# Layer 0 of a hybrid decoder step: a plain first chunk of 256 tokens, and the Strassen weight sums of the second chunk on GpSimd

## The chip, the cores and the metric

The kernel runs on one core of a Trainium2 chip. The metric is the device time of one execution in microseconds (us). Of the kernel before three runs are shown; their median counts. The engines are TensorE (PE in the profile, its weight loads PEld), VectorE (DVE), ScalarE (ACT), GpSimd (POOL) and SyncE (SP), which here only issues DMAs, in order.

## The reference

The step has two layers over 4096 prompt tokens and 8 sample tokens of width 1024. Only layer 0 is touched. It is, in short:

```python
def even_layer(x, pool_prefix, conv_prefix, pos0, g_norm, w_in, pool_w, pool_scale, conv_w, w_out):
    h = rms_norm(x, g_norm)                       # x * rsqrt(mean(x*x) + eps) * g_norm
    p = jnp.einsum('btd,de->bte', h, w_in)        # 1024 -> 3072
    u, z_a, b_gate, c_gate, v_in, z_b = jnp.split(p, EVEN_SPLITS, axis=-1)
    d = pool_mix(u, pool_prefix, pos0).reshape(B, T, N_POOL_GROUPS, POOL_GROUP)   # windows 2, 4, 8, 16
    y_a = jnp.einsum('btgc,gce->btge', d, pool_w).reshape(B, T, W_POOL) * pool_scale * jax.nn.silu(z_a)
    v = c_gate * v_in
    y_b = b_gate * short_conv(v, conv_prefix, conv_w) * jax.nn.silu(z_b)
    y = jnp.einsum('bte,ed->btd', jnp.concatenate([y_a, y_b], axis=-1), w_out)
    return x + y, new_pool, new_conv
```

Layer 1 is sliding-window attention with its own projections. All is float32.

## The kernel before, in words

Every float32 operand of a product is split in two float32r parts, high and low (`split`: ScalarE copies the high part, VectorE subtracts), and a product takes three matmuls: high by high, high by low, low by high.

Layer 0 takes the tokens in chunks (`L0_CHUNKS`): 768, 768, 768, 768, 512, 512; the 8 samples ride with the first. For each chunk:

- `prep` loads the token tiles, normalizes them (`x_norm0`: ScalarE squares, GpSimd makes the root, VectorE scales), turns them by TensorE transposes and makes the seven token operands of a Strassen-Winograd product: B11, B21, B22 and the sums T1 to T4, split in `bh`, `bl`, `th`, `tl`. It works in rounds of 256 tokens; the two halves of a chunk are the two columns of the Strassen square.
- `mixers` runs 12 pairs of output blocks of 128 channels (4 groups, 3 pairs each). A pair is 7 products of 4 x 3 matmuls with half the chunk's tokens as columns: 84 matmuls of 384 columns (388 in chunk 0, 256 in the small chunks). Its weight operands are A11, A12 (one block), the sums S1 to S4, and A22, 3.5 tiles of 128x1024 to be split per pair. In chunk 0 `operands` loads both blocks from `w_in`, GpSimd multiplies them by the norm's gains (`scaled`), VectorE makes three sums and GpSimd one, and all seven are written to a scratch tensor `wsc`; later chunks load them from there. Between the products stand the evictions, the pooling, the convolution and the gates, on VectorE, ScalarE and, for small copies, GpSimd.
- `outproj` multiplies by `w_out` in 8 weight blocks: 3 x 8 x 2 matmuls of 512 columns for every 128 tokens, adds the input and writes the result for layer 1.

Raw weight tiles (`wr`), high parts (`wh`) and low parts (`wl`) have three buffers each, token tiles and weight sums share two (`x`), the operands of a chunk and its `yh`, `yl` have one. A scheduler orders the instructions of each engine at build time by their dependences and its own estimates; so `prep` of the next chunk, which stands between `mixers` and `outproj` in the code, comes out mixed with the output projection. Layer 1 follows from 1498 us on.

Of the kernel before, what the change touches and what calls it, by code (L numbers as in the profile page):

```python
# [54 lines left out]
def hybrid_kernel(  # L55
# [94 lines left out]
    with ExitStack() as l1:  # L150
# [119 lines left out]
        def x_norm0(xt, n, junk):  # L270
# [4 lines left out]
            dve.tensor_scalar(out=xt[:n], in0=xt[:n], scalar1=r[:n, 0:1], scalar2=None, op0=ALU.mult)  # L275

        def prep(ci):
# [39 lines left out]
            for i in range(np2):  # L317
                xs = []
                for j in (1, 0):
                    if early:  # L320
                        xt = early.pop(0)
                    else:
                        xt = xp.tile([P, D], F32, tag="x", name="xt", bufs=2)
                        r0 = t0 + j * (n // 2) + i * P
# [12 lines left out]
                operand_cols(i * P, P, quad)  # L337
            if ci == 0:
                xs1 = xp.tile([P, D], F32, tag="x", name="xs1", bufs=2)
                sp.dma_start(xs1[:NS], xs_flat)  # L340
                sj = xp.tile([P, KT, P], F32, tag="x", name="sj", bufs=2)
                x_norm0(xs1, NS, sj)
                v = samples_to_channels(xs1, pt)
                h = NS // 2
                operand_cols(n // 2, h, lambda k, j: v[:, 4 * k:4 * k + 4, j * h:j * h + h])
            return bh, bl, th, tl

        def mixers(ci, X, yh, yl):
            t0, n = L0_CHUNKS[ci]
            L = n // 2  # L350
            hs = NS // 2 if ci == 0 else 0
            w = L + hs
            bh, bl, th, tl = X
            B = {"B11": (bh, bl, 0), "B21": (bh, bl, 1), "B22": (bh, bl, 2), "T1": (th, tl, 0),
                 "T2": (th, tl, 1), "T3": (th, tl, 2), "T4": (th, tl, 3)}
# [46 lines left out]
            WX = w  # L402

            def put_y(kt, pi, fn):
                y = tp.tile([P, WX], F32, tag="dy", name="y")
# [1 line left out]
                cs = slice(pi * L, pi * L + L)
                split(yh[:, kt, cs], yl[:, kt, cs], y[:, :L])
                if hs:
                    ss_ = slice(n + pi * hs, n + pi * hs + hs)  # L410
                    split(yh[:, kt, ss_], yl[:, kt, ss_], y[:, L:w])

            for g in range(4):
                win = 2 << g
                us = [tp.tile([P, 15 + WX], F32, tag="uv", name="u") for _ in range(2)]
# [8 lines left out]

                def pooled(pi):
# [985 lines left out]
```

## Time and profile before

| | |
|---|---|
| median of 3 runs | 3348.16 us (3347.56 to 3349.6) |
| profiled execution, its own time | 3354.14 us |
| its span, first to last instruction | 3352.4 us |
| TensorE busy | 3131.0 us, 93% |
| VectorE busy | 2471.7 us, 74% |
| ScalarE busy | 1892.4 us, 56% |
| GpSimd busy | 860.1 us, 26% |
| mean granted TensorE clock | 0.981 |

TensorE is the busiest engine, so a change pays where TensorE waits, or where it is given less or faster work. A busy share over the whole span hides that: layer 0 has stretches with TensorE at over 99% and others at a quarter. So the rows further down cut layer 0 where TensorE turns from one kind of work to the next. Matmul durations overlap, since they are pipelined; what a matmul costs is the length of a full stretch divided by its matmuls.

### The profile page before, as it was taken

The numbers are of one execution on the slowest core, as the hardware profiler recorded it, in microseconds if no ns is written. First come the engines' busy times: TensorE is split into PE (matmuls) and PEld (weight loads), VectorE is DVE, ScalarE is ACT, GpSimd is POOL, SyncE is SP. The second block draws the span as 40 slices with busy tenths as digits, with TensorE's granted clock in tenths as the row PEclk, the third lists the DMA queues.
The fourth block names the chain that finished last, engine by engine and source line by source line (L and its number), as shares of the span: only waits on it lengthen the run. The fifth ranks groups of instructions, "written<-read, shape, count | busy, mean of one in ns | idle before, by whom it ended". The sixth has DMA issues, their size and how long they took to land.

```text
span 3352.4 us, 48712 instructions
## 1 busy us (share of the span) xinstructions
PE 3131.0 (93%) x16362; PEld 2687.0 (80%) x16362; DVE 2471.7 (74%) x4914; ACT 1892.4 (56%) x4277; POOL 860.1 (26%) x1219
## 2 busy tenths in 40 slices
PE   4889999999999999998989999999999999999877
PEld 3887898898899898976767777777787777776665
DVE  5896467467467486853897987979979788797863
ACT  4334345245244254544686876858858688585761
POOL 2441011011011011110333442534425334243420
PEclk9999999999999999999999999999999999999988
DMA  4554444534543555553213324233242242322212
GB/s 135 173 170 140 149 123 134 160 120 129 164 126 121 171 176 180 176 176 111 88 53 103 113 76 138 73 103 114 74 138 79 89 128 71 120 70 63 70 64 98
DMA packets 220997, 398.90 MB, mean 119 GB/s; under 512 B 25257, under 2 KB 89393, under 8 KB 220706
## 3 DMA queue, kind: packets, MB, share of 16 engines
q1 hardware_dynamic: 220745, 395.78, 37.6%
q8 instruction: 129, 2.11, 0.3%
q14 instruction: 123, 1.00, 0.1%
HBM read 339.70 MB, written 58.31 MB: 119 GB/s over the span
## 4 chain that ended last, share of the span: by engine, by line
PE 23%; DVE 15%; ACT 7%; DMA 5%; issue 3%; POOL 1%; SPq 1%; DVEq 0%; ACTq 0%; POOLq 0%
PE pst L720 6%; PE pst L721 6%; PE pst L722 6%; ACT s L989 3%; DVE wl L688 2%; DMA wr<-in_w_in_odd_dram 2%; DVE qt L72 1%; PE o L1023 1%; DVE s L973 1%; DMA xr<-x 1%; PE sc L965 1%; DMA out_dram<-xr 1%; DVE st L983 1%; DVE ot L75 1%; ACT wh L687 1%
## 5 line engine op out<-in xcount | busy, mean ns | idle before, releaser
L69 ACT ACTIVATE wh<-wr 128x512 fp32r<-128x512 f32 (+1 forms) x392 | 327.6, 840 | 448.5 <-PE pz L373 125.0
L72 DVE TENSOR_TENSOR wl<-wr,wh 128x512 fp32r<-128x512 f32 (+1 forms) x392 | 373.2, 960 | 214.9 <-ACT wh L69 194.0
L688 DVE SCALAR_TENSOR_TENSOR wl<-wr,gt,wh 128x256 fp32r<-128x256 f32 (+1 forms) x448 | 277.3, 637 | 69.5 <-ACT wh L687 67.5
L687 ACT ACTIVATE wh<-wr,gt 128x256 fp32r<-128x256 f32 (+1 forms) x448 | 250.3, 596 | 120.6 <-DMA wr<-in_w_in_odd_dram 80.3
L720 PE MATMUL pst<-wh,hh 128*128 128x512 f32 x768 | 312.0, 406 | 1.7 <-DVE xr L75 1.7
L722 PE MATMUL pst<-wl,hh 128*128 128x512 f32 x768 | 304.4, 396 | 0.0
L721 PE MATMUL pst<-wh,hl 128*128 128x512 f32 x768 | 304.2, 396 | 0.0
L373 PE MATMUL px<-th,wh 128*128 128x384 f32 (+2 forms) x864 | 280.1, 324 | 9.8 <-DVE za L75 6.4
L373 PE MATMUL px<-th,wl 128*128 128x384 f32 (+2 forms) x864 | 278.7, 323 | 0.0
L373 PE MATMUL px<-tl,wh 128*128 128x384 f32 (+2 forms) x864 | 278.7, 323 | 0.0
L1009 POOL TENSOR_SCALAR_AFFINE_SELECT qh<-ph 128x512 fp32r<-128x512 f32 x124 | 88.7, 715 | 692.5 <-ACT ph L69 675.4
L989 ACT ACTIVATE s<-s,st,rq 128x128 f32<-128x128 f32 x512 | 246.8, 483 | 33.8 <-DVE st L985 32.3
L808 PE MATMUL psz<-hh,wh 128*128 128x512 f32 x512 | 213.5, 417 | 9.8 <-ACT wh L687 9.8
L720 PE MATMUL pst<-wh,yh 128*128 128x512 f32 x512 | 211.2, 413 | 2.6 <-DVE xr L75 2.6
L570 PE MATMUL pso<-who,yh 128*128 128x512 f32 x512 | 204.7, 400 | 5.6 <-DVE xr L75 5.5
L809 PE MATMUL psz<-hl,wh 128*128 128x512 f32 x512 | 208.7, 408 | 0.0
L810 PE MATMUL psz<-hh,wl 128*128 128x512 f32 x512 | 207.6, 405 | 0.0
L721 PE MATMUL pst<-wh,yl 128*128 128x512 f32 x512 | 204.3, 399 | 0.0
L572 PE MATMUL pso<-who,yl 128*128 128x512 f32 x512 | 204.3, 399 | 0.0
L722 PE MATMUL pst<-wl,yh 128*128 128x512 f32 x512 | 204.2, 399 | 0.0
L574 PE MATMUL pso<-wlo,yh 128*128 128x512 f32 x512 | 202.7, 397 | 0.0
L428 POOL COPY ucar<-u 128x15 f32<-128x15 f32 x48 | 26.4, 550 | 611.0 <-DVE u L75 599.2
(327 smaller groups left out, 9038.6 us busy)
## 6 DMA issues: line engine op xcount, KB each, us to landing
wr<-wsc SPq DMA_DIRECT2D x180, 512.0 KB
wr<-in_w_in_odd_dram SPq DMA_DIRECT2D x320, 256.0 KB
wr<-in_w_out_odd_dram SPq DMA_DIRECT2D x128, 256.0 KB
wro<-in_w_out_even_dram SPq DMA_DIRECT2D x48, 512.0 KB
xr<-in_x_prompt_dram SPq DMA_DIRECT2D x64, 256.0 KB
x<-xr SPq DMA_DIRECT2D x64, 256.0 KB
xt<-x SPq DMA_DIRECT2D x32, 512.0 KB
xr<-x SPq DMA_DIRECT2D x64, 256.0 KB
```

The lines of the kernel that those rows point to most:

```text
L69: return act.activation(out, in_, AF.Copy)
L72: return dve.tensor_tensor(out=out, in0=a, in1=b, op=ALU.subtract)
L373: pe.matmul(ps, lhsT=u_[:, at, kt, :], rhs=v_[:, o, kt, :], start=start and kt == 0 and i == 0, stop=kt == 3 and i == 2, skip_group_check= ...
L687: act.activation(wh[ix], raw[ix], AF.Copy, scale=gt[:, kt:kt + 1])
L688: dve.scalar_tensor_tensor(out=wl[ix], in0=raw[ix], scalar=gt[:, kt:kt + 1], in1=f(wh[ix]), op0=ALU.mult, op1=ALU.subtract)
L720: pe.matmul(acc[i], lhsT=xh(kt), rhs=wh, start=kt == 0, stop=False)
L721: pe.matmul(acc[i], lhsT=xl(kt), rhs=wh, start=False, stop=False)
L722: pe.matmul(acc[i], lhsT=xh(kt), rhs=wl, start=False, stop=kt == KT - 1)
L808: pe.matmul(acc[e], lhsT=wh[:, k, es], rhs=xh, start=kt == 0, stop=False)
L809: pe.matmul(acc[e], lhsT=wh[:, k, es], rhs=xl, start=False, stop=False)
L810: pe.matmul(acc[e], lhsT=wl[:, k, es], rhs=xh, start=False, stop=kt == KT - 1)
L989: C["exp"] = act.activation(s[:, h, :], s[:, h, :], AF.Exp, bias=nm[:, h:h + 1], scale=r4[:, h:h + 1], accum_out=den[:, h:h + 1])
```

## The change

The chunks become one of 256 tokens and five of 768. The first chunk, with the samples, is a plain product: no Strassen operands, 24 weight blocks of 24 matmuls each with 264 columns, 576 in place of 1008 of half width. Its split tokens, its y and the samples' strip all lie in the buffers of `yh` and `yl`, so `bh`, `bl`, `th`, `tl` stay free for chunk 1. The norm's gains go to the tokens instead of the weights: a tile `gb` holds them for every partition, and `x_norm0` multiplies by both in one scalar_tensor_tensor. The second chunk makes the weight sums, all four on GpSimd, and writes only these to `wsc`; the blocks themselves are loaded from `w_in` in every chunk.

```diff
-L0_CHUNKS = [(0, 768), (768, 768), (1536, 768), (2304, 768), (3072, 512), (3584, 512)]
+L0_CHUNKS = [(0, 256)] + [(256 + 768 * i, 768) for i in range(5)]
...
-        wsc = [dram.tile([P, 7, 4, P], F32, tag=f"wsc{i}", name=f"wsc{i}") for i in range(12)]
+        wsc = [dram.tile([P, 4, 4, P], F32, tag=f"wsc{i}", name=f"wsc{i}") for i in range(12)]
...
-        g0 = c1.tile([P, KT], F32, tag="g0", name="g0")
+        gb = c1.tile([P, D], F32, tag="gb", name="gb")
...
-        def scaled(raw):
-            v = raw.rearrange("p a k e -> p (a k) e")
-            pool.tensor_tensor(out=v, in0=v, in1=g0.unsqueeze(2).to_broadcast([P, KT, P]),
-                               op=ALU.mult)
-
         first_w = []
 
+        def block_parts(eb):
+            return parts(first_w.pop(0) if first_w else load_block(eb))
+
         def operands(ci, pair, blocks):
 
-            if ci > 0:
-                out = []
-                for i in range(4):
+            ra = load_block(blocks[0])
+            ga = parts(ra)
+            if ci > 1:
+                out = [ga]
+                for i in range(2):
                     raw = raw_tile()
-                    n = 1 if i == 3 else 2
-                    sp.dma_start(raw[:, :n], wsc[pair][:, 2 * i:2 * i + n])
-                    out.append(parts(raw[:, :n]))
+                    sp.dma_start(raw, wsc[pair][:, 2 * i:2 * i + 2])
+                    out.append(parts(raw))
+                raw = raw_tile()
+                e0 = blocks[1] * P
+                sp.dma_start(raw[:, 0], w_in[:, 4:8, e0:e0 + P])
+                out.append(parts(raw[:, 0:1]))
                 return out
-            ra = first_w.pop(0) if first_w else load_block(blocks[0])
-            scaled(ra)
-            ga = parts(ra)
-            rb = first_w.pop(0) if first_w else load_block(blocks[1])
-            scaled(rb)
+            rb = load_block(blocks[1])
             s12 = xp.tile([P, 2, 4, P], F32, tag="x", name="s12", bufs=2)
             s34 = xp.tile([P, 2, 4, P], F32, tag="x", name="s34", bufs=2)
-            add(s12[:, 1], rb[:, 0], rb[:, 1])
-            sub(s12[:, 0], s12[:, 1], ra[:, 0])
+            pool.tensor_tensor(out=s12[:, 1], in0=rb[:, 0], in1=rb[:, 1], op=ALU.add)
+            pool.tensor_tensor(out=s12[:, 0], in0=s12[:, 1], in1=ra[:, 0], op=ALU.subtract)
+            gs12 = parts(s12)
             pool.tensor_tensor(out=s34[:, 0], in0=ra[:, 0], in1=rb[:, 0], op=ALU.subtract)
-            sub(s34[:, 1], ra[:, 1], s12[:, 0])
-            sp.dma_start(wsc[pair][:, 0:2], ra)
-            gs12 = parts(s12)
-            sp.dma_start(wsc[pair][:, 2:4], s12)
+            pool.tensor_tensor(out=s34[:, 1], in0=ra[:, 1], in1=s12[:, 0], op=ALU.subtract)
+            sp.dma_start(wsc[pair][:, 0:2], s12)
             gs34 = parts(s34)
-            sp.dma_start(wsc[pair][:, 4:6], s34)
-            gb_ = parts(rb[:, 1:2])
-            sp.dma_start(wsc[pair][:, 6:7], rb[:, 1:2])
-            return [ga, gs12, gs34, gb_]
+            sp.dma_start(wsc[pair][:, 2:4], s34)
+            return [ga, gs12, gs34, parts(rb[:, 1:2])]
...
             r = rstd(ss[:n], n, 1, 1.0 / D, EPS, sm, "rn")
-            dve.tensor_scalar(out=xt[:n], in0=xt[:n], scalar1=r[:n, 0:1], scalar2=None, op0=ALU.mult)
+            dve.scalar_tensor_tensor(out=xt[:n], in0=xt[:n], scalar=r[:n, 0:1], in1=gb[:n],
+                                     op0=ALU.mult, op1=ALU.mult)
+
+        def prep0():
+
+            n = L0_CHUNKS[0][1]
+            both = [yp.tile([P, KT, 2 * (n + NS) + 40], F32R, tag=t, name=f"{t}0") for t in ("yh", "yl")]
+            hh, hl = (t[:, :, 0:n + NS] for t in both)
+            yh, yl = (t[:, :, n + NS:2 * (n + NS)] for t in both)
+            ysk = both[0][:, :, 2 * (n + NS):]
+            for i in range(n // P):
+                xt = early[i]
+                x_norm0(xt, P, yl[:, :, 0:P])
+                to_channels(xt, pt, hh, hl, i * P)
+            x_norm0(early[-1], NS, yl[:, :, P:2 * P])
+            v = samples_to_channels(early[-1], pt)
+            split(hh[:, :, n:n + NS], hl[:, :, n:n + NS], v)
+            return hh, hl, yh, yl, ysk
...
+                if plain:
+                    for e in range(2):
+                        wh, wl = block_parts(blocks[e])
+                        ps = bank("ps")
+                        for kt in range(KT):
+                            for k, (u_, v_) in enumerate(((wh, hh), (wh, hl), (wl, hh))):
+                                pe.matmul(ps, lhsT=u_[:, kt // 4, kt % 4, :], rhs=v_[:, kt, :],
+                                          start=kt == 0 and k == 0, stop=kt == KT - 1 and k == 2)
+                        if e == 0:
+                            out11(ps, None)
+                            if mid is not None:
+                                mid()
+                    return ps
...
         early = []
-        for i, r0 in enumerate((384, 0)):
+        for i in range(2):
             xt = xp.tile([P, D], F32, tag="x", name="xe", bufs=2)
-            sp.dma_start(xt, xp_flat[r0:r0 + P, :])
+            sp.dma_start(xt, xp_flat[i * P:(i + 1) * P, :])
             early.append(xt)
-        with nc.allow_non_contiguous_dma(reason="per-channel gains"):
-            sp.dma_start(g0, norm_g[0].rearrange("(k p) -> p k", p=P))
-        first_w += [load_block(0), load_block(4)]
-        nxt = prep(0)
+            if i == 0:
+                sp.dma_start(gb, norm_g[0].partition_broadcast(P))
+                first_w.append(load_block(0))
+        xs1 = wp.tile([P, D], F32, tag="wr", name="xs1", bufs=3)
+        sp.dma_start(xs1[:NS], xs_flat)
+        early.append(xs1)
+        first_w.append(load_block(4))
+        hh, hl, yh0, yl0, ysk0 = prep0()
         setup()
```

The remaining edits make one list entry of two where the chunk is plain (`NP`), and copy from PSUM where there is no second summand.

At the head, VectorE's first rows before were (`xe`, `xt` token tiles, `rnr` the root, `wr` a raw weight tile, `bl`, `tl` low parts):

```order
L275 TENSOR_SCALAR xe<-xe,rnr 128x1024 x2
L72 TENSOR_TENSOR wl<-wr,wh 128x1024
L72 TENSOR_TENSOR bl<-tr,bh 128x4x128
L72 TENSOR_TENSOR t_190<-b_176,tr 128x512
L72 TENSOR_TENSOR bl<-tr,bh 128x4x128
L72 TENSOR_TENSOR t_199<-tr,t_190 128x512
L72 TENSOR_TENSOR tl<-t_190,th 128x4x128
L72 TENSOR_TENSOR bl<-tr,bh 128x4x128
```

and now, where `xs` are the samples and the split tokens lie in `yh`, `yl`:

```order
L72 TENSOR_TENSOR wl<-wr,wh 128x1024
L271 SCALAR_TENSOR_TENSOR xe<-xe,rnr,gb 128x1024 x2
L271 SCALAR_TENSOR_TENSOR xs_156<-xs_156,rnr,gb 8x1024
L72 TENSOR_TENSOR yl_161<-tr,yh_160 128x4x128
L72 TENSOR_TENSOR wl<-wr,wh 128x1024
L72 TENSOR_TENSOR yl_161<-tr,yh_160 128x4x128 x2
L72 TENSOR_TENSOR pwl<-pw,pwh 128x512
L72 TENSOR_TENSOR yl_161<-tr,yh_160 128x4x128
L72 TENSOR_TENSOR yl_161<-trs,yh_160 128x8x8
L75 TENSOR_TENSOR nx<-u 128x270
```

The first weight block's split stands ahead of the scaling now, and three scalings and the splits of two tiles make the whole of it; before, two more rounds of eleven operations follow.

At the start of the output projection TensorE's rows before were (`tr` transposes of the next chunk's tokens, `pso` outputs of the projection, `who`, `wlo` its split weights):

```order
L574 MATMUL pso<-wlo,yh 128x512
L570 MATMUL pso<-who,yh 128x512
L334 MATMUL tr<-ident,xt 128x128 x4
L572 MATMUL pso<-who,yl 128x512
L574 MATMUL pso<-wlo,yh 128x512
L570 MATMUL pso<-who,yh 128x512
L572 MATMUL pso<-who,yl 128x512
L574 MATMUL pso<-wlo,yh 128x512
L570 MATMUL pso<-who,yh 128x512
L572 MATMUL pso<-who,yl 128x512
L574 MATMUL pso<-wlo,yh 128x512
```

and now, a few rows further on, where 4 + 6 + 4 + 12 + 4 + 1 + 4 + 17 such matmuls and transposes lie behind (`pss` are the samples):

```order
L592 MATMUL pso<-who,yh_160 128x512
L594 MATMUL pso<-who,yl_161 128x512
L596 MATMUL pso<-wlo,yh_160 128x512
L344 MATMUL tr<-ident,xt 128x128 x32
L601 MATMUL pss<-who,yh_160 40x512
L603 MATMUL pss<-wlo,yh_160 40x512
L601 MATMUL pss<-who,yh_160 40x512
L603 MATMUL pss<-wlo,yh_160 40x512
L601 MATMUL pss<-who,yh_160 40x512
L603 MATMUL pss<-wlo,yh_160 40x512
L601 MATMUL pss<-who,yh_160 40x512
```

Before, transposes alternate with some ten output matmuls all the way; now the last two rounds' 32 transposes stand in one run, and the samples' and the remaining output matmuls follow them.

On GpSimd the weight work of the chunk that makes the sums was, in chunk 0 (`wr` scaled by `g`, `s` a sum, `vv`, `u` tiles that get a few carried columns):

```order
L197 TENSOR_TENSOR wr<-wr,g_139 128x1024 x2
L221 TENSOR_TENSOR s_612<-wr 128x512
L197 TENSOR_TENSOR wr<-wr,g_139 128x1024
L496 COPY vv<-vcar 128x2
L221 TENSOR_TENSOR s_782<-wr 128x512
L197 TENSOR_TENSOR wr<-wr,g_139 128x1024
L497 COPY vcar<-vv 128x2
L496 COPY vv<-vcar 128x2
L497 COPY vcar<-vv 128x2
```

and is now, in chunk 1:

```order
L218 TENSOR_TENSOR s_1656<-wr 128x512
L221 TENSOR_TENSOR s_1657<-wr 128x512
L219 TENSOR_TENSOR s_1656<-s_1656,wr 128x512
L222 TENSOR_TENSOR s_1657<-wr,s_1656 128x512
L218 TENSOR_TENSOR s_1806<-wr 128x512
L221 TENSOR_TENSOR s_1807<-wr 128x512
L219 TENSOR_TENSOR s_1806<-s_1806,wr 128x512
L222 TENSOR_TENSOR s_1807<-wr,s_1806 128x512
L449 COPY ucar<-u 128x15
L448 COPY u<-ucar 128x15
L449 COPY ucar<-u 128x15
L218 TENSOR_TENSOR s_1960<-wr 128x512
```

The scaling is gone, a pair has four sums instead of one, and the sums of two pairs run before the first copy that waits for a product. On SP the second state load, `sc_raw`, now has two loads of weight blocks right behind it, and the two copies of the caches stand among the weight loads of the first chunk; before, these copies were issued at 33.34 and 42.12 us, ahead of the products.

## Rows read from the trace of the kernel before

**Rows 1.** Busy time of each engine by stretch, cut where TensorE's work changes.
```profile
core 0: us, PE busy (x) PEld busy (x) DVE busy (x) ACT busy (x) POOL busy (x), PEclk, DMA share, GB/s
0.00:53.50 53.50, 13.38 (x56) 9.92 (x56) 30.27 (x43) 24.27 (x43) 14.88 (x44) 1.00 0.53 167
77.50:92.20 14.70, 5.04 (x16) 2.88 (x16) 9.41 (x14) 3.78 (x14) 5.64 (x3) 0.57 0.53 154
92.20:283.10 190.90, 174.98 (x920) 170.84 (x921) 163.16 (x273) 71.69 (x123) 71.45 (x58) 0.94 0.50 168
...
283.10:314.50 31.40, 29.58 (x155) 23.50 (x154) 24.31 (x43) 20.92 (x39) 6.01 (x12) 1.00 0.34 116
314.50:368.60 54.10, 52.25 (x222) 38.61 (x221) 19.54 (x25) 10.05 (x12) 0.00 (x0) 1.00 0.48 148
368.60:550.50 181.90, 181.82 (x1034) 180.99 (x1033) 125.20 (x193) 80.55 (x123) 19.62 (x32) 1.00 0.44 134
550.50:627.40 76.90, 73.31 (x337) 58.40 (x336) 41.81 (x61) 29.01 (x47) 5.92 (x12) 1.00 0.46 148
...
809.30:888.20 78.90, 75.08 (x339) 59.78 (x338) 41.95 (x61) 29.16 (x47) 5.91 (x12) 0.98 0.46 144
...
1069.90:1146.90 77.00, 71.54 (x321) 56.97 (x320) 33.80 (x48) 22.48 (x35) 3.69 (x8) 1.00 0.43 134
1146.90:1274.70 127.80, 126.33 (x1034) 123.39 (x1033) 104.11 (x191) 70.40 (x122) 17.92 (x32) 1.00 0.61 189
...
1452.60:1498.20 45.60, 45.60 (x203) 36.98 (x202) 16.45 (x25) 12.08 (x22) 2.84 (x9) 1.00 0.46 151
```

**Rows 2.** Timeline of the head: start us, us, engine, line, tiles, [idle before <-releaser].
```profile
8.29 1.90 POOL L197 TENSOR_TENSOR wr<-wr,g 128x1024 f32<-128x1024 f32 x1 [2.41 <-DMA wr<-in_w_in_even_dram]
...
23.86 0.69 DVE L72 TENSOR_TENSOR tl<-t,th 128x512 fp32r<-128x512 f32 x1 [0.69 <-ACT th L69]
...
48.83 0.69 DVE L72 TENSOR_TENSOR tl<-t,th 128x512 fp32r<-128x512 f32 x1 [0.69 <-ACT th L69]
...
53.54 0.69 PE L373 MATMUL px<-bh,wh 128*128 128x388 f32 x1 [0.41 <-ACT bh L69]
...
56.94 0.53 PE L373 MATMUL px<-bl,wh 128*128 128x388 f32 x1
57.26 0.53 PE L373 MATMUL px<-bh,wl 128*128 128x388 f32 x1
```

**Rows 3.** Waits from 53 to 283 us: in total, times, longest us.
```profile
POOL wr L197 <- DMA wr<-in_w_in_even_dram: 54.4, 11, 11.3
```

**Rows 4.** Timeline of one weight load of chunk 0, issue and first use.
```profile
92.60 3.40 SPq L192 DMA_DIRECT2D wr<-in_w_in_even_dram  x2
...
97.38 1.90 POOL L197 TENSOR_TENSOR wr<-wr,g 128x1024 f32<-128x1024 f32 x1 [8.03 <-DMA wr<-in_w_in_even_dram]
```

**Rows 5.** Groups by line and form, 0 to 1500 us: count, busy us, mean ns, idle before.
```profile
L72 DVE TENSOR_TENSOR wl<-wr,wh 128x1024 fp32r<-128x1024 f32 x192 | 237.1, 1235 | 150.3 <-ACT wh L69 149.5
...
L69 ACT ACTIVATE wh<-wr 128x1024 fp32r<-128x1024 f32 x192 | 203.4, 1059 | 274.5 <-PE pz L373 125.0 <-PE pso L572 69.4 <-PE px L373 28.0
...
L197 POOL TENSOR_TENSOR wr<-wr,g 128x1024 f32<-128x1024 f32 x24 | 54.4, 2267 | 82.7 <-DMA wr<-in_w_in_even_dram 57.1 <-DVE t L78 5.7 <-DVE t L499 4.2
...
L275 DVE TENSOR_SCALAR xt<-xt,rnr 128x1024 f32<-128x1024 f32 x30 | 22.6, 753 | 22.0 <-POOL rnr L109 21.1 <-ACT who L69 0.7
...
L221 POOL TENSOR_TENSOR s<-wr 128x512 f32<-128x512 f32 x12 | 18.7, 1556 | 9.0 <-issue 4.1 <-DVE wl L72 2.6 <-PE trs L138 2.0
...
L437 DVE SCALAR_TENSOR_TENSOR d<-nx,u 128x384 f32<-128x384 f32 x32 | 17.8, 557 | 0.8
...
L72 DVE TENSOR_TENSOR dl<-d,dh 128x384 fp32r<-128x384 f32 x24 | 13.4, 557 | 11.0 <-ACT dh L69 11.0
...
L72 DVE TENSOR_TENSOR dl<-d,dh 128x388 fp32r<-128x388 f32 x8 | 10.6, 1332 | 1.1 <-ACT dh L69 1.1
```

**Rows 6.** Timeline of TensorE, the last transposes of chunk 1's operands.
```profile
313.91 0.60 PE L334 MATMUL tr<-ident,xt 128*128 128x128 f32 x4
```

More of the change, by code (lines that the diff above doesn't have):

```diff
@@ L335, in quad @@
                     return tr
[L337 to L345, printed above, removed]
+                operand_cols(i * P, quad)
             return bh, bl, th, tl
@@ L349, in mixers @@
             t0, n = L0_CHUNKS[ci]
[L350 to L355, printed above, removed]
+            plain = ci == 0
+            NP = 1 if plain else 2
+            L = n // NP
+            hs = NS if plain else 0
+            w = WX = L + hs
+            if plain:
+                hh, hl = X
+            else:
+                bh, bl, th, tl = X
+                B = {"B11": (bh, bl, 0), "B21": (bh, bl, 1), "B22": (bh, bl, 2), "T1": (th, tl, 0),
+                     "T2": (th, tl, 1), "T3": (th, tl, 2), "T4": (th, tl, 3)}
             last = ci == len(L0_CHUNKS) - 1
@@ L400, in pair, with plus @@
                 return x
-            WX = w
+            def plus(out, a, b):
+                if b is None:
+                    acopy(out, a)
+                else:
+                    add(out, a, b)
             def put_y(kt, pi, fn):
@@ L406, in put_y @@
                 fn(y)
[L407 to L411, printed above, removed]
+                cs = slice(pi * L, pi * L + w)
+                split(yh[:, kt, cs], yl[:, kt, cs], y)
             for g in range(4):
                 win = 2 << g
-                us = [tp.tile([P, 15 + WX], F32, tag="uv", name="u") for _ in range(2)]
-                zs = [tp.tile([P, WX], F32, tag="z", name="za") for _ in range(2)]
+                us = [tp.tile([P, 15 + WX], F32, tag="uv", name="u") for _ in range(NP)]
+                zs = [tp.tile([P, WX], F32, tag="z", name="za") for _ in range(NP)]
                 def into_u(pi):
                     def fn(a, b):
-                        add(us[pi][:, 15:15 + L], a[:, :L], b[:, :L])
+                        plus(us[pi][:, 15:15 + L], a[:, :L], b)
                         if hs:
-                            add(stp[:, g, pi * hs:pi * hs + hs, 15], a[:, L:w], b[:, L:w])
+                            acopy(stp[:, g, :, 15], a[:, L:w])
                     return fn
@@ L457, in into @@
                 def into(t):
-                    return lambda a, b: add(t, a, b)
+                    return lambda a, b: plus(t, a, b)
                 def silu_(t, src):
@@ L468, in mixers @@
                 silu_(zs[0], c21)
-                ds_ = [pooled(0), pooled(1)]
+                ds_ = [pooled(pi) for pi in range(NP)]
                 def linear():
-                    for pi in range(2):
+                    for pi in range(NP):
                         ps = bank("psd")
@@ L480, in linear @@
                             op1=ALU.mult))
-                cs_ = [tp.tile([P, WX], F32, tag="c", name="c") for _ in range(2)]
-                vs = [tp.tile([P, 15 + WX], F32, tag="uv", name="vv") for _ in range(2)]
+                cs_ = [tp.tile([P, WX], F32, tag="c", name="c") for _ in range(NP)]
+                vs = [tp.tile([P, 15 + WX], F32, tag="uv", name="vv") for _ in range(NP)]
                 def out_v2(a, b):
                     add(vs[1][:, 2:2 + w], a, b)
-                c21 = pair(3 * g + 1, (12 + g, 16 + g), into(cs_[0]), into(cs_[1]), out_v2, linear)
+                c21 = pair(3 * g + 1, (12 + g, 16 + g), into(cs_[0]), into(cs_[-1]), out_v2, linear)
                 ts_ = []
-                for pi in range(2):
+                for pi in range(NP):
                     vv, c = vs[pi], cs_[pi]
@@ L517, in fn @@
                         z = tp.tile([P, WX], F32, tag="z", name="zb")
-                        add(z, a, b)
-                        silu_(z, z)
+                        if b is None:
+                            silu_(z, a)
+                        else:
+                            add(z, a, b)
+                            silu_(z, z)
                         mul(ts_[pi], ts_[pi], z)
@@ L530, in mixers @@
                 put_y(4 + g, 0, lambda o: mul(o, c21, ts_[0]))
-                y2 = ys[0]
-                mul(y2, y2, ts_[1])
-                split(yh[:, 4 + g, L:n], yl[:, 4 + g, L:n], y2[:, :L])
-                if hs:
-                    split(yh[:, 4 + g, n + hs:n + NS], yl[:, 4 + g, n + hs:n + NS], y2[:, L:w])
+                if not plain:
+                    y2 = ys[0]
+                    mul(y2, y2, ts_[1])
+                    split(yh[:, 4 + g, L:n], yl[:, 4 + g, L:n], y2)
             def tails(src, n_rows, dst):
```

42 lines of the change are left out of this document (22 added, 20 removed).

## The prediction, made before the changed kernel ran

> **What bounds the kernel now.** I read the busy times by stretch first, cut where TensorE turns from one kind of work to the next [rows 1]. Layer 0 lies in 0 to 1498.2 us of the 3352.4 us span; layer 1, with TensorE 93% busy, is not edited. In layer 0 the chunks after the first are bound by TensorE: 181.8 of 181.9 us busy in chunk 1's products (three chunks like it agree within 0.2 us), 126.3 of 127.8 in chunk 4's (the other small chunk takes 127.0). So there only matmuls count. Idle TensorE lies in three places: the head, 53.5 us with 13.4 busy; chunk 0's products, 229.6 us (53.5 to 283.1) where the same products take 181.9 in chunk 1; and, small, the stretches in which the output projection is mixed with the next chunk's operands (76.9 us with 73.3 busy). Then I read the timeline of the head, the waits of chunk 0, and the durations by form.
>
> The head is a chain: three rounds of 256 tokens through ScalarE, VectorE and the transposes, the last split at 48.83 us, then the samples; first product at 53.5 [rows 2]. It starts at the half clock: 388 columns in 0.32 us, that is 1.2 GHz. Chunk 0's products lose time in two ways: a stop from 77.5 to 92.2 for the state rows (5.0 us of 14.7 busy), and from 92.2 on 15.9 us idle and a clock of 0.94 [rows 1]. What is late there is the weights: a load issued at 92.60 is first used at 97.38, GpSimd then scales each block (2267 ns, 24 of them), and waits 54.4 us for loads in all [rows 3 to 5].
>
> **The change part by part.** The sum is made by stages of TensorE, against the profiled execution: 3352.4 us of span, 3354.14 us in all. The median of the runs shown, 3348.16, is 6.0 lower; I take the difference from the median.
>
> Matmul pitch first. A small chunk has 1008 products and 24 small ones of 256 columns in 127.8 us, 0.1238 us each; chunk 1 has as many of 384 in 181.9, 0.1763. So 0.00041 us a column, and 0.127 for the 264 columns of the plain chunk. An output matmul of 512 takes 45.6/192 = 0.2375.
>
> *Head.* Before: 53.5. After: two token tiles and the samples only. By the order VectorE now splits weight block 0 before it scales the tokens, and this block must have landed. It was in use at 8.29 as the fourth transfer and is third now, behind the 512 KB gain row. From 8.3: split on ScalarE 1.06 and VectorE 1.24, three scalings by a tensor_tensor's time (1.24 each, below), then in VectorE's order four token splits (0.69 each), one block (1.24), the pooling weights (0.69) and a small one: 8.3 + 2.3 + 3.7 + 4.9 = 19.2. I take 19.5. Bounds: 16 if nothing queues, 26 by before's first round, whose last split ends at 24.55 [rows 2].
>
> *Chunk 0's products.* 576 plain plus 12 small matmuls at 0.127: 74.8. The half clock at the start: before it held for 9 us; 41 matmuls at 0.22 instead of 0.127, 3.8. The stop for the state rows: the second state load waits for a tile that TensorE frees after block 1, and two weight loads stand behind it on SP. Before, the loads at that place took from 77.5 to 92.2; now the first state row is there in time, so I take 5, and 4 for the clock after it. Pair by pair, before lost 26.6 us over 11 pairs to gaps and clock (15.9 idle and some 10.7 for the 0.94). The scaling and VectorE's sums, which made splits late, are gone, but a block is needed every 3.05 us instead of 3.5 splits every 14.8: I take 0.95 a pair, 10.4 (bounds 0 and 26.6). The two cache copies of 1016 KB move from the head to among the weight loads; at the head's 167 GB/s each could hold a load up by 6 us, of which two spare buffers hide nearly all: 2 together. Sum 100, against 229.6.
>
> *Output projection 0 with chunk 1's operands.* Before 85.5 (31.4 to the last transposes [rows 6], 54.1 after). Now only 96 + 32 matmuls stand against the same three rounds. TensorE's order puts 36 of them in the first round and then 32 transposes in one go, so TensorE mostly waits for 20 us, and 92 matmuls come behind. The rounds: 31.4, and 1.9 for four scalings in the chain that are now scalar_tensor_tensor. That form is not in the trace at 1024 columns. Bounds: 0.75 (the tensor_scalar it replaces) and 1.24 (tensor_tensor); at 384 columns both two-input forms take 0.557 [rows 5], so 1.24. Then 92 × 0.2375 = 21.9, 2.5 for the fourth weight block, whose split stands behind the operands', and 4 for a clock that fell in the idle part: 61.7. The samples' matmuls are unchanged, and the four later preparations hide their longer scaling behind more output matmuls.
>
> *Chunk 1's products with the weight sums on GpSimd.* 181.9 if TensorE alone counts. Four GpSimd sums of 128x512 a pair at 1.56 us are 6.2 of a pair's 14.8 us, and by the order they run one pair ahead, so the chain is hidden. What isn't is VectorE: where GpSimd ran beside it, a split of 388 columns took 1332 ns, one of 384 columns 557 [rows 5]. From 92.2 to 283.1 VectorE was busy 163 us. Chunk 1's 125 scaled by 920 of 1034 matmuls is 111; 11 pairs of three sums at 0.69 add 23, the samples' short operations some 13 (estimate: 16 of 0.2 a group): 147. So GpSimd's 67 us of reads (22 scalings, 11 sums) added about 16. For chunk 1 that is 125 + 16 of 182: still cover. I take 6 for late splits, 188 (bounds 182 and 212).
> The Trainium skill, SBUF — State Buffer, section "Who interferes with whom", says that a VectorE instruction with two SBUF inputs and a GpSimd one that reads SBUF block each other for the whole instruction. The pair of 1332 and 557 ns agrees; that GpSimd's whole time is lost does not, since 67 us cost about 16. By the rule at its full price chunk 1 is a rival, below.
>
> *The rest.* Chunks 2 to 5 are all of 384 columns: 4 × 181.8 = 727.3 (their loads carry as many bytes). Output projections 1 to 4 of 768 tokens with operands: the mean of 76.9, 78.9 and 77.0, so 4 × 77.6 = 310.4; the last has none behind it: 288 × 0.2375 = 68.4. Before, these were 181.9 + 181.9 + 181.7, 232.8, 254.8 and 96.5 us. More products in plain form and fewer, wider ones elsewhere nearly cancel: 19,008 more columns at 0.00041 cost 7.8, and 432 fewer matmuls save 432 × 0.019 = 8.2.
>
> Layer 0 after: 19.5 + 100 + 61.7 + 188 + 727.3 + 310.4 + 68.4 = 1475.3, against 1498.2: 22.9 less. TensorE's order in layer 1 is the same, so its time stays. 3348.2 - 22.9 = 3325.3; I say 3325.
>
> **Rivals.**
> *Weights pace the plain chunk (slower).* A block costs load, two splits and release: 4.8 + 1.06 + 1.24 = 7.1 us a buffer; with three in flight 2.4 us, with TensorE's 3.05 deciding. If SP's queue, in order, lets only one and a half overlap, a block takes 4.7: 24 × 1.65 = 40 more, 3365. It decides from 4.0 us a block on, where the gain is gone. For: ScalarE's splits wait behind evictions. Against: chunk 4 takes 48 loads (42 full ones) in 127.8 us, 3.05 per full block, with TensorE 99% busy [rows 1]. Chance 0.12.
> *GpSimd's reads stop VectorE for their whole time.* 125 + 48 × 1.56 = 200 in chunk 1, and with what waits for it 205 to 215: 17 to 27 worse than forecast, 3342 to 3352. For: the 1332 ns. Against: the 16 us above. The rule of the Trainium skill cited above (SBUF — State Buffer) is this mechanism. Chance 0.12.
> *The plain chunk runs nearly without stops* and the sums cost nothing: 10 + 4 + 4 + 6 off, 3301. For: VectorE needs some 15 of a group's 18.7 us (six splits of 1.24, some 17 operations of 0.45). Against: the half clock has followed every stop so far. Chance 0.14.
> *Forecast*, 3310 to 3340: 0.62.
>
> **How the numbers follow.** The bounds of the head (-4, +7), chunk 0 (-14, +20), chunk 1 (-6, +24) and some 8 for the exposed rounds, not all at once, give the forecast its ±15; the rivals take the range to 3299 and 3353. A measurement of this kernel tells a change from none at 0.2%, 6.7 us. The forecast, the good rival and a little of the GpSimd rival are faster: 0.78. GpSimd's upper half and the milder weight cases are the same: 0.10. Weights at over 4.3 us a block and pile-ups are slower: 0.12.
>
> **What would show it.** First product near 19.5 us; chunk 0's last at about 120; 20 us of sparse transposes after it; chunk 1's products at about 181, ending at 369; chunk 5's at the pitch of 0.176. Wrong if TensorE in the plain chunk waits on weight splits block after block, or VectorE is over 95% busy in chunk 1, or the head ends after 26 us.

## The result, and the profile after

The changed kernel takes 3310.84 us (median of 4, 3309.86 to 3315.95) against 3347.86 for the kernel before (4 runs): ratio 0.9894, 95% interval 0.9877 to 0.9911. Its profiled execution took 3315.95 us, with a span of 3314.2 (3352.4 before). Layer 0 ends at 1461.1 us instead of 1498.2; layer 1 takes 1853.1 instead of 1854.2. So the change lies in layer 0, as forecast, and is larger: 37 us, where the forecast said 23.

The stretches after, cut in the same way as [rows 1] (columns: engine busy us and instruction count, granted clock, DMA share, GB/s):

```profile
core 0: us, PE busy (x) PEld busy (x) DVE busy (x) ACT busy (x) POOL busy (x), PEclk, DMA share, GB/s
0.00:20.80 20.80, 5.20 (x25) 3.98 (x25) 9.25 (x11) 9.64 (x15) 5.72 (x33) 1.00 0.59 152
20.80:107.00 86.20, 80.00 (x606) 77.98 (x607) 56.21 (x113) 39.44 (x70) 7.00 (x19) 0.96 0.68 205
107.00:138.60 31.60, 18.16 (x85) 13.73 (x82) 23.54 (x36) 17.86 (x31) 3.73 (x8) 0.71 0.30 101
138.60:163.60 25.00, 22.90 (x93) 15.58 (x93) 14.70 (x19) 10.14 (x12) 5.72 (x4) 0.89 0.49 148
163.60:375.00 211.40, 191.59 (x1034) 187.87 (x1033) 154.86 (x192) 79.52 (x123) 82.31 (x76) 0.95 0.40 133
375.00:449.50 74.50, 72.38 (x337) 58.01 (x336) 45.11 (x61) 29.21 (x46) 7.50 (x12) 1.00 0.46 152
449.50:629.20 179.70, 179.62 (x1034) 179.00 (x1033) 124.07 (x191) 79.61 (x123) 19.26 (x32) 1.00 0.42 137
629.20:704.60 75.40, 72.12 (x338) 58.08 (x337) 45.19 (x61) 29.27 (x47) 7.88 (x12) 1.00 0.45 150
...
1394.20:1461.10 66.90, 66.56 (x296) 54.44 (x295) 18.52 (x28) 12.39 (x22) 2.82 (x9) 1.00 0.38 121
```

| stage, us | before | predicted | after |
|---|---|---|---|
| head | 53.5 | 19.5 | 20.8 |
| chunk 0's products | 229.6 | 100 | 86.2 |
| output projection 0 | 85.5 | 61.7 | 56.6 |
| chunk 1's products | 181.9 | 188 | 211.4 |
| products of chunks 2 to 5 | 618.4 | 727.3 | 720.3 |
| output projections 1 to 4 | 283.7 | 310.4 | 298.9 |
| last output projection | 45.6 | 68.4 | 66.9 |

(Before, chunk 0 and its output projection hold 776 tokens, the last two chunks 512 each; after, 264 and 768.) The forecast came out near because its errors have both signs: chunk 1 is 23.4 worse, the stages beside it 38.9 better, the head 1.3 worse.

Chunk 1 is the row to look at. TensorE does the same 1034 matmuls as in chunk 2, but 19.8 us are idle (211.40 - 191.59), and 12.0 more are busy than there (191.59 - 179.62) at a clock of 0.95. VectorE is busy 30.8 us longer, with the same work. GpSimd's 82 us hold some 70 of sums. TensorE's waits there (in total, times, longest us) are these:

```profile
PE px L393 <- ACT u L69: 8.0, 3, 4.6
PE pz L393 <- ACT p L69: 7.4, 4, 2.1
PE psd L496 <- ACT dh L69: 3.0, 2, 2.1
PE psd L497 <- DVE dl L72: 1.4, 3, 0.6
```

They are all of the 19.8 us: waits for evictions (`u`, `p`) and for the operand of the pooling's product (`dh`, `dl`), none for a split of weights. Which VectorE instructions grow? Chunk 1's products by form (count, busy us, mean ns, idle before):

```profile
L72 DVE TENSOR_TENSOR wl<-s,wh 128x1024 fp32r<-128x1024 f32 x24 | 35.9, 1497 | 6.6 <-ACT wh L69 6.6
L523 DVE SCALAR_TENSOR_TENSOR t<-vv,cw,t 128x384 f32<-128x384 f32 x16 | 17.5, 1120 | 0.0
...
L72 DVE TENSOR_TENSOR wl<-wr,wh 128x512 fp32r<-128x512 f32 x12 | 11.3, 942 | 0.0
...
L75 DVE TENSOR_TENSOR u<-pz,u 128x384 f32<-128x384 f32 x4 | 2.2, 558 | 5.3 <-PE pz L393 5.3
```

and in chunk 2, where GpSimd adds nothing:

```profile
L72 DVE TENSOR_TENSOR wl<-wr,wh 128x1024 fp32r<-128x1024 f32 x34 | 41.5, 1222 | 20.9 <-ACT wh L69 20.9
L523 DVE SCALAR_TENSOR_TENSOR t<-vv,cw,t 128x384 f32<-128x384 f32 x16 | 8.8, 608 | 0.0
L72 DVE TENSOR_TENSOR wl<-wr,wh 128x512 fp32r<-128x512 f32 x12 | 8.2, 683 | 0.0
...
L75 DVE TENSOR_TENSOR u<-pz,u 128x384 f32<-128x384 f32 x4 | 2.2, 558 | 3.5 <-PE pz L393 3.5
```

The convolution's scalar_tensor_tensor goes from 608 to 1120 ns, a half-width weight split from 683 to 942. The add with one input in PSUM (`pz`) keeps its 558. Then I followed one stop of TensorE back, the longest (4.59 us), in the timeline (start, us, engine; `zb` a gate's input, `u` an eviction):

```profile
201.50 1.29 POOL L218 TENSOR_TENSOR s<-wr 128x512 f32<-128x512 f32 x1 [7.33 <-DMA wr<-in_w_in_even_dram]
...
202.87 1.28 POOL L219 TENSOR_TENSOR s<-s,wr 128x512 f32<-128x512 f32 x1
...
204.10 0.19 POOL L517 COPY vv<-vcar 128x2 f32<-128x2 f32 x1
...
204.32 0.42 DVE L520 TENSOR_SCALAR t<-vv,cw 128x384 f32<-128x384 f32 x1 [5.07 <-POOL vv L517]
...
204.66 3.15 DVE L523 SCALAR_TENSOR_TENSOR t<-vv,cw,t 128x384 f32<-128x384 f32 x2
205.82 1.57 POOL L222 TENSOR_TENSOR s<-wr,s 128x512 f32<-128x512 f32 x1
...
207.73 0.54 DVE L75 TENSOR_TENSOR zb<-py,p 128x384 f32<-128x384 f32 x1
...
208.31 0.52 ACT L482 ACTIVATE zb<-zb 128x384 f32<-128x384 f32 x1 [7.30 <-DVE zb L75]
...
208.74 0.47 ACT L69 ACTIVATE u<-px 128x384 f32<-128x384 f32 x1
```
```profile
209.26 0.69 PE L393 MATMUL px<-th,wh 128*128 128x384 f32 x1 [4.59 <-ACT u L69]
```

Read from the end: the matmul waits for ScalarE's eviction, this stands behind a gate that waits for VectorE's add, the add behind the convolution, the convolution waits for a copy of two carried columns on GpSimd, and the copy stands behind a weight sum that waited 7.33 us for its load. In the same place the two convolution steps take 3.15 us beside GpSimd's adds, not 1.2. So there are two suspects: GpSimd's in-order queue, and a resource that both engines read by.

### The profile page after: what moved, and what is told of

It reads as the page before. It is cut to its first block, busy times and chain, and to the rows that moved or that the text cites. A ratio compares the mean times of both kernels' runs of the same rounds, so it can differ in the third digit from the quotient of the medians.

```text
span 3314.2 us, 47323 instructions
## 1 busy us (share of the span) xinstructions
PE 3111.7 (94%) x15918; PEld 2678.9 (81%) x15918; DVE 2423.0 (73%) x4699; ACT 1861.8 (56%) x4182; POOL 855.6 (26%) x1215
## 4 chain that ended last, share of the span: by engine, by line
PE 56%; DVE 19%; ACT 9%; DMA 7%; issue 6%; POOL 2%; SPq 1%; DVEq 0%; ACTq 0%; POOLq 0%
PE px L393 13%; PE pz L393 7%; PE pst L751 6%; PE pst L752 6%; PE pst L753 6%; PE py L393 3%; ACT s L1020 3%; DVE wl L719 2%; PE pso L594 2%; PE pso L596 2%; PE pso L592 2%; DMA wr<-in_w_in_odd_dram 2%; DVE qt L72 1%; PE o L1054 1%; PE sc L996 1%
## 5 line engine op out<-in xcount | busy, mean ns | idle before, releaser
L69 ACT ACTIVATE wh<-wr 128x1024 fp32r<-128x1024 f32 (+1 forms) x368 | 306.8, 839 | 432.5 <-PE pz L393 110.9
L72 DVE TENSOR_TENSOR wl<-wr,wh 128x1024 fp32r<-128x1024 f32 (+1 forms) x368 | 350.2, 962 | 220.5 <-ACT wh L69 210.0
L393 PE MATMUL px<-th,wh 128*128 128x384 f32 x720 | 243.9, 339 | 9.7 <-ACT u L69 8.0
L393 PE MATMUL px<-tl,wh 128*128 128x384 f32 x720 | 243.2, 338 | 0.0
L393 PE MATMUL px<-th,wl 128*128 128x384 f32 x720 | 243.1, 338 | 0.0
L753 PEld LDWEIGHTS pst<-wl,hh 128*128 128x128 f32 x768 | 144.6, 188 | 35.0
```

Of the source, the lines that this page charges most:

```text
L69: return act.activation(out, in_, AF.Copy)
L72: return dve.tensor_tensor(out=out, in0=a, in1=b, op=ALU.subtract)
L393: pe.matmul(ps, lhsT=u_[:, at, kt, :], rhs=v_[:, o, kt, :], start=start and kt == 0 and i == 0, stop=kt == 3 and i == 2, skip_group_check= ...
L753: pe.matmul(acc[i], lhsT=xh(kt), rhs=wl, start=False, stop=kt == KT - 1)
```

## The experiments

Ratios are against the kernel before on the same chip; 0.001 is 3.35 us. Stage times are from one profile of each run, with rows as in the stretches above; from run to run, stages that were not edited differ by up to 1.5 us. The first five tell the two suspects of chunk 1 apart; the others price the rest of the change.

**Sums on VectorE.**

```diff
-pool.tensor_tensor(out=s12[:, 1], in0=rb[:, 0], in1=rb[:, 1], op=ALU.add)
+add(s12[:, 1], rb[:, 0], rb[:, 1])          # and the other three alike
```


> The changed kernel with all four weight sums of chunk 1 on VectorE instead of GpSimd; nothing else is edited. Theory 1 (GpSimd's sums stop VectorE's instructions of two SBUF inputs, and hold GpSimd's carry copies in its queue, and both make evictions late): chunk 1's products fall from 211.4 us to 181-188, the GpSimd copies wait for nothing long, the time falls by 23-30 us to about 3285. Theory 2 (VectorE's total work is what counts: 124 us of its own and 44 sums of 0.69 = 30 make 154, as much as the 155 it shows now): chunk 1 stays at 205-212 and the time within 6 us of 3311. Theory 3 (the chain of two loads, sums and splits through three buffers is late, whichever engine adds): 200 us or more.

3290.25 us, ratio 0.9817 (0.9800 to 0.9835), 26 us less than the changed kernel by the ratios. Chunk 1, and one of the sums on VectorE:
```profile
164.10:344.00 179.90, 179.90 (x1034) 179.00 (x1033) 146.69 (x234) 80.04 (x124) 27.17 (x32) 1.00 0.45 150
...
L75 DVE TENSOR_TENSOR s<-wr 128x512 f32<-128x512 f32 x11 | 7.5, 683 | 3.5 <-DMA wr<-in_w_in_even_dram 2.6 <-DVE vv L78 0.5 <-DVE d L458 0.4
```
Theory 1 holds; 2 and 3 are out. VectorE has the 44 sums of this stretch on top (234 instructions instead of 192) and yet less busy time than in the changed kernel (146.7 against 154.9), and TensorE has no stop left. The placing of the sums on GpSimd cost 31.5 us of products.

**Three sums on VectorE, one on GpSimd**, as the kernel before has it (only L221 stays `pool.`).

> The changed kernel with three of chunk 1's sums on VectorE and one (the first of s34) on GpSimd, as before the change. If what costs grows with GpSimd's time (four sums cost 211.4 - 179.9 = 31.5 us), one sum costs a quarter, chunk 1 takes 186-190 us, and the time is 3296-3301. If it takes the chain of four (a carry copy that has to let two sums and a load by) the one sum costs under 3 us: 180-183, 3290-3293.

3293.75 us, 0.9827 (0.9810 to 0.9844); chunk 1 184.6 us. It falls between the two expectations: the cost, 4.7 us, grows with GpSimd's time, but less than in proportion (a quarter would be 7.9).

**Carry copies on ScalarE** in chunk 1.

```diff
-pool.tensor_copy(vv[:, 0:2], vcar[:, g, :])
+(acopy if ci == 1 else pool.tensor_copy)(vv[:, 0:2], vcar[:, g, :])   # and three more
```


> The changed kernel with the four small carry copies of chunk 1 (15 and 2 columns, 32 in all) on ScalarE instead of GpSimd; the sums stay on GpSimd. If the queue is what costs (carry copies that stand behind sums, and these behind a weight load), the two to five us stops at the third pair of each group go and chunk 1's products take 185-195 us, 3290-3297 in all. If the stopped VectorE instructions cost by themselves, chunk 1 stays at 203-212 us and the time within 8 us of 3311, and the convolution's scalar_tensor_tensor stays near 1.1 us in the mean.

3307.87 us, 0.9870 (0.9855 to 0.9885). Chunk 1:
```profile
165.00:366.30 201.30, 185.74 (x1034) 182.00 (x1033) 159.62 (x193) 84.42 (x156) 68.89 (x46) 0.98 0.44 140
```
Taking the copies out of GpSimd's queue was worth about a third (10.1 of 31.5 us), so that the run falls between the two expectations, close to the second; the larger part is still there. The convolution's scalar_tensor_tensor takes 837 ns in the mean, not the 1.1 us of the second expectation, while VectorE as a whole is busy longer than in the changed kernel (159.6 against 154.9): which instructions are held depends on what they meet.

**Adds that nothing waits for.**

```diff
+            spare = stp.rearrange("p g b r -> p (g b r)").rearrange("p (k e) -> p k e", e=P)
+            for wh, wl in (gs12, gs34):
+                for a in range(2):
+                    pool.tensor_tensor(out=spare, in0=f(wh[:, a]), in1=f(wl[:, a]), op=ALU.add)
```


> The version with the sums on VectorE and with chunk 1's carry copies on ScalarE, and besides, behind each pair's weight splits, four GpSimd adds of 128x512 of the split weights into a tile that nothing reads any more: as much GpSimd time as the change's sums take, with the same two SBUF inputs, but no instruction waits for them. If GpSimd's reads alone stop VectorE (the part of the 31.5 us that the carry copies do not explain, 21), VectorE's two-input instructions lengthen and chunk 1's products rise from 179.9 to 192-208 us, 3303-3318 in all. If it was the chain (two loads, four sums and a split, one behind the other), chunk 1 stays at 180-185 us and 3290-3296.

3317.82 us, 0.9899 (0.9882 to 0.9915). Chunk 1, and two groups in it:
```profile
164.90:375.90 211.00, 187.39 (x1034) 181.65 (x1033) 186.27 (x234) 83.34 (x155) 70.64 (x49) 0.98 0.39 128
```
```profile
L75 DVE TENSOR_TENSOR s<-wr 128x512 f32<-128x512 f32 x11 | 16.5, 1503 | 5.0 <-DMA wr<-in_w_in_even_dram 2.7 <-issue 1.6 <-DVE nx L75 0.8
...
L75 DVE TENSOR_TENSOR u<-pz,u 128x384 f32<-128x384 f32 x4 | 2.2, 556 | 0.8 <-PE pz L397 0.8
```
This is the run that decides. No instruction waits for the adds' results, no carry stands behind them, and yet 31.1 us come back, with VectorE busy 39.6 us longer, both against the version with the sums on VectorE (which keeps its carry copies on GpSimd; one with them on ScalarE and without the adds was not run). A sum of 128x512 on VectorE takes 1503 ns here and 683 there. One other path is small: three weight splits on ScalarE waited, 7.0 us in all, for buffers that the adds were still reading, and none of TensorE's waits is for a weight split. The expectation's upper end, 208, was too low; here VectorE also has the 44 sums, more instructions that can be held than in the changed kernel, so the 31.1 us show that the mechanism is enough and not what its share was.

**Copies instead of adds** (`pool.tensor_copy(spare, f(wl[:, a]))`).

> The same with copies of 128x512 (one SBUF input) on GpSimd in the place of the adds. If only instructions of two inputs on both engines block each other, chunk 1 stays at 180-185 us and VectorE's durations at those of the version without; if any GpSimd read does, it lies between that and the run with adds, by the copies' share of the adds' time.

3291.86 us in one run; chunk 1 186.7 us.
```profile
163.50:350.20 186.70, 181.56 (x1034) 178.72 (x1033) 158.24 (x234) 84.30 (x155) 45.11 (x48) 1.00 0.44 148
```
Copies with one input in SBUF hold VectorE up too (11.5 us more busy; whether by their reads or their writes is not separated), and cost 6.8 us for 45 of copies: less than the adds by their time's share (45 of 72 us would be 19). Why an add's microsecond costs more than a copy's was not tried.

**Scaling taken out of the kernel before** (the gains are left out).

```diff
-            scaled(ra)
...
-            scaled(rb)
```


> The kernel before without the scaling of chunk 0's weight blocks by the gains on GpSimd (24 instructions of 2.27 us; the gains are left out of the result), chunks and sums as before. If the scaling was most of what chunk 0 lost: its products fall from 229.6 us to 195-205, and the time from 3348 to 3315-3323, so that most of the change's gain in chunk 0 could be had without the plain product. If the VectorE sums and the late state rows were most of it: 215-229 us and 3335-3348.

3325.54 us, 0.9924 (0.9909 to 0.9939), which is 3323 from a start of 3348.
```profile
47.80:252.40 204.60, 192.76 (x1043) 188.74 (x1044) 161.99 (x313) 85.11 (x154) 31.75 (x44) 0.97 0.53 174
```
The first expectation holds. Chunk 0's products lose 25.0 us and the head 5.7, and VectorE's busy time there falls from 183.4 to 162.0: 54 us of scaling on GpSimd had held VectorE for 21. (The way from a load to its split is shorter too; how the 25.0 us divide between the two is not shown.) Over layer 0 this makes 29 us (1469.2 instead of 1498.2; 25 by the medians of the runs), without any plain chunk; in the changed kernel the tokens' longer scaling stands against it, which the output projections hide.

**Operand tiles back at the old addresses** (`bh`, `bl`, `th` 388 columns wide, used at a pitch of 384; `tl`, the last of them, keeps its new size, since there is no room for all four).

```diff
+        def padded(tag, k, N):
+            t = hp.tile([P, k * 4 * (N + 4)], F32R, tag=tag, name=tag)
+            return t[:, :k * 4 * N].rearrange("p (a b n) -> p a b n", a=k, b=4)
```


> The changed kernel with the tiles bh, bl and th allocated 388 columns wide as before (used at a row pitch of 384), so that bl, th and tl start at the byte addresses that they had before; yh and yl shift by 640. Theory placement (where the operand tiles start sets the pitch of products that alternate between them): the pitch of 384 columns goes from a uniform 173 ns back to the pattern of 169, 176 and 182 that the products from bh and bl show before, chunks 2 to 5 from 180 to 181.8-182.3 us each, and the time rises by 8 to 12 us (to 3319-3323), up to 19 if the output projections' 227 goes back to 232 as well. Rival (the pitch depends on the weight loads, half of which are now 512-byte pieces): pitch stays 173, time within 4 us of 3311.

3326.24 us, 0.9926 (0.9909 to 0.9943), 11 us slower than the changed kernel by the ratios. Chunk 2, its output projection, and the last one:
```profile
447.50:629.10 181.60, 181.60 (x1034) 181.13 (x1033) 124.43 (x191) 79.82 (x123) 19.31 (x32) 1.00 0.43 135
629.10:704.60 75.50, 73.16 (x337) 58.11 (x336) 45.08 (x61) 29.19 (x47) 8.59 (x12) 1.00 0.46 151
1401.60:1470.70 69.10, 68.10 (x296) 54.62 (x295) 18.46 (x28) 12.38 (x22) 2.83 (x9) 1.00 0.37 117
```
Placement holds. From the starts of consecutive matmuls of 384 columns, the pitch is 173 or 174 ns throughout in the changed kernel; here it is spread from 168 to 182 again, as before, where those of `py` took 176, 182 and 169 by turns of operands.

**The kernel before with its operand tiles aligned** (18,944 and 25,088 bytes a partition).

```diff
+            t = hp.tile([P, {3: 4736, 4: 6272}[k]], F32R, tag=tag, name=tag)
```


> The kernel before, with bh and bl allocated 18944 bytes a partition and th and tl 25088, so that all operand tiles start at the same place within 512 bytes; contents, loads and order as before. Theory placement: the pitch of 384 columns goes from 169/176/182 to a uniform 173, chunks 1 to 3 from 182 to 180 us each, and the time falls by 6 to 12 us from 3350. Rival (loads or the chunk plan): pitch and time stay within 4 us.

3344.63 us, 0.9982 (0.9972 to 0.9993). Chunk 1:
```profile
367.50:547.30 179.80, 179.80 (x1034) 179.06 (x1033) 125.08 (x194) 80.48 (x124) 19.66 (x32) 1.00 0.43 135
```
Chunks 1 to 3 take 179.8, 180.8 and 180.3 us instead of 182.0, at a pitch of 173. The same effect from the other side, at the low end of what was expected; the chunks of 256 columns gain nothing (128.4 and 127.7).

**Sums on VectorE, and chunk 1's operands made among chunk 0's products.**

```diff
+                if plain and g:
+                    next(steps1)        # one round of 256 tokens of prep(1)
                 c21 = pair(3 * g + 1, (12 + g, 16 + g), into(cs_[0]), into(cs_[-1]), out_v2, linear)
```


> The version with the sums on VectorE, and besides with chunk 1's operands made among the plain chunk's products (one round of 256 tokens in each of groups 1 to 3) instead of beside output projection 0. If the 20 us of sparse transposes there are only a chain with nothing beside it, chunk 0 with its output projection falls from 143 us (85.5 and 57.6) to 120-128 and the time from 3290 to 3268-3277. Rival (VectorE, 56 of 86 us busy in the plain chunk, is given 28 more and now paces the weight splits): the products of chunk 0 take 105-115 us, the sum stays at 135-145, and the time within 7 us of 3290.

3267.74 us, 0.9751 (0.9733 to 0.9769): the fastest version, 43 us below the changed kernel by the medians and 48 by the ratios. The first expectation holds: 127.0 us from the first product to the projection's end, where it was 143.
```profile
21.00:114.10 93.10, 84.99 (x624) 82.75 (x625) 73.51 (x142) 55.04 (x99) 12.21 (x27) 0.95 0.66 201
114.10:148.00 33.90, 33.48 (x159) 24.86 (x157) 21.21 (x30) 11.45 (x14) 0.00 (x0) 1.00 0.64 198
```
The three rounds add 7.6 us to the products and take 23.7 from the projection, in which TensorE is now busy 33.5 of 33.9 us. VectorE, at 79%, does not pace the plain chunk.

## Why the prediction was right, and where its steps were not

*Head* (19.5 predicted, 20.8 measured): right, by its own chain, where [rows 2] had three rounds. VectorE's first block split, at 9.57 us, is ahead of the tokens as the order said, and the first product starts at 20.75:
```profile
9.57 1.23 DVE L72 TENSOR_TENSOR wl<-wr,wh 128x1024 fp32r<-128x1024 f32 x1 [9.57 <-ACT wh L69]
...
20.15 0.69 DVE L72 TENSOR_TENSOR yl<-tr,yh 128x512 fp32r<-128x512 f32 x1 [0.44 <-ACT yh L69]
...
20.75 0.81 PE L376 MATMUL ps<-yh,wh 128*128 128x264 f32 x2 [0.31 <-ACT yh L69]
```

*Chunk 0's products* (100, 86.2): within the bounds, each term too high. A product of 264 columns takes 0.122 us, not 0.127: 71.7 instead of 74.8 for the matmuls. The idle time, state rows and all, is 6.2 us where 5 + 10.4 + 2 were set aside. At the start 16 products took 0.22 us each, where 41 were expected, and after that the clock fell twice only, for 3.4 us each (the second fall below; 0.50 is 1.2 GHz):
```profile
75.80:79.20 3.40, 3.40 (x18) 3.40 (x17) 2.19 (x3) 0.93 (x1) 0.00 (x0) 0.50 0.76 218
```
TensorE's waits from 20.8 to 107 us (in total, times, longest):
```profile
PE ps L376 <- ACT wh L69: 2.6, 2, 1.4
PE tr L260 <- DMA sc_raw<-in_state_conv_dram: 1.9, 1, 1.9
PE ps L376 <- DVE wl L72: 1.1, 2, 0.8
```
Weight splits cost 3.7 us in all, so weights do not pace the plain chunk: the slower rival fell, and that of a plain chunk nearly without stops was right for this stage. The argument held against it, that the half clock had followed every stop, was misread. In this stretch of chunk 0 of before, TensorE stopped three times for 1.0 to 1.2 us, and the granted clock stayed at 1.00:
```profile
196.00:250.00 54.00, 50.51 (x281) 49.19 (x280) 48.63 (x81) 21.31 (x37) 23.14 (x18) 1.00 0.48 161
```

*Output projection 0* (61.7, 56.6): the mechanism is right. The sparse part takes 31.6 us, with TensorE busy 18.2; behind it come 25.0 us, where 28.4 were set. That it is a chain with nothing beside it, the last experiment shows.

*Chunk 1* (188, 211.4) is the step that failed: "I take 6 for late splits". The rival "GpSimd's reads stop VectorE for their whole time", with 205 to 215, had this stage right. The path was wrong: TensorE waited for evictions and the pooling's operand, and for no late split of weights. So was the sign that I had named, VectorE over 95% busy: it was at 73% while the stage lost its time. Two sub-steps made the price wrong. The price was calibrated on chunk 0 of before [rows 1, 5]: 147 us of VectorE's own need, so that 67 us of reads cost 16. The run without scaling shows 162.0 with 12 GpSimd sums still there, of 183.4: 54 us of scaling alone cost 21, and at that rate the sums' 75 us would have cost 29. And the cover was counted as a sum (141 of 182 us). With the copies off GpSimd VectorE lost 35.5 us (159.6 against the 124.1 of chunk 2) and TensorE still 21.4: the idle time makes up for part only, since lengthened instructions stand in the chain from product to eviction, as the stop that was followed shows. With the stops the clock fell six times in the stage, for 3.4 us each. What I had not looked for is the queue: the carry copies behind the sums.

The Trainium skill, SBUF — State Buffer, "Who interferes with whom", says that a VectorE instruction with two SBUF inputs contends with a GpSimd instruction that reads SBUF, and that one with at most one SBUF input (outside its two-port modes) does not. The runs agree: 608 to 1120 ns with two, 558 and 558 with one in PSUM. A tensor_scalar with one tensor input in SBUF grew as well, from 418 ns in the version with the sums on VectorE to 1011 beside the adds that nothing waits for; whether it ran in a two-port mode no row here shows. Weighed by its full price, as a rival, it would have given 200 and more for the stage, where the prediction took the milder reading of one comparison.

*Chunks 2 to 5 and the output projections* (727.3 and 378.8, 720.3 and 365.8): the pitch was taken from before as a property of the columns, 0.1763 and 0.2375 us; after, it is 0.174 (179.7/1034) and 0.232 (66.9/288). The tiles moved: `bh` and `bl` shrank from 18,624 bytes (36 x 512 + 192) to 18,432 (36 x 512), `th` and `tl` from 24,832 to 24,576, so all operand tiles start at the same place within 512 bytes. Both placement runs show this as a cause; the padded one puts about 13 of the 20 us down to it: without chunk 1, its layer 0 is 13.2 longer (9.6 in all, with chunk 1 3.6 shorter). The other 7 or so lie in the output projections beside `prep`: 75.5 us even with the tiles put back, where 77.6 was the mean of three of before; that was not taken further.

*The median* stands at the lower end of the forecast's own range, 3310 to 3340, by errors that cancel. Of the gain of 37.1 us in layer 0, by these runs, some 29 come from taking the gains off the weights, 13 from placement, some 25 from the plain chunk and the new sizes (38.2 from the run without scaling to that with sums on VectorE, less the 13), and 30 were given back by the sums on GpSimd. The parts were not all run alone from one base, so this is a sum of differences, good to a few us.

## What to carry to other kernels

Before work is moved to GpSimd because VectorE seems the busier, look at what both read: adds on GpSimd lengthened VectorE's work by about half of the adds' own time (30.8 us for 70, 39.6 for 72), and the same adds cost less on VectorE itself (0.68 us against 1.5). A small copy that a chain needs should not share an in-order queue with work that waits for a load. When a change alters tile sizes, compare the pitch of matmuls in a stretch that was not edited: here that gave a third of the gain, and the change was not made for it.

## What had not been expected of the hardware

In these kernels the matmul pitch depends on where the operand tiles start in SBUF: some 169, 176 or 182 ns for 384 columns when the starts differ within 512 bytes, 173 or 174 when they agree. Which step of alignment is enough, and by which path, was not tried.

The block between VectorE and GpSimd goes both ways. In chunk 2 of the changed kernel, where no engine makes sums, four of the eight copies of 15 columns on GpSimd take 0.42 us and the other four 2.26. One of these four, and VectorE beside it:
```profile
483.67 2.26 POOL L448 COPY u<-ucar 128x15 f32<-128x15 f32 x1 [1.86 <-DVE t L523]
...
481.94 2.19 DVE L523 SCALAR_TENSOR_TENSOR t<-vv,cw,t 128x384 f32<-128x384 f32 x4
484.06 1.82 DVE L72 TENSOR_TENSOR wl<-wr,wh 128x1024 fp32r<-128x1024 f32 x2
485.79 0.55 DVE L75 TENSOR_TENSOR zb<-py,p 128x384 f32<-128x384 f32 x1
```
The copy begins while the convolution runs and ends at 485.93 us, 0.05 after the second split, when VectorE has turned to an add with an input in PSUM; the other three run in the same way. So instructions of two SBUF inputs that follow each other closely held it for all of their time. In the version with one GpSimd sum the eight copies take 1.9 us in the mean, in chunk 1 of the changed kernel 0.66: there three of the four that are held in chunk 2 come right behind the sums, and take 0.53.
